# Masked softmax: later loads in quarter tiles of one packet per DMA engine, whole-tile stores, an earlier start of GpSimd's loads

## The chip, the cores and the metric

The kernel runs on one core of a Trainium2 chip. The metric is the device time of one execution in microseconds (us); the time of a kernel is the median of its runs. The profile of one execution gives a span a little shorter than that time (155.8 us for a run of 158.12 us), and all places in time below count from the span's start.

## The reference

```python
def setup_inputs():
    batch, heads, seq_q, seq_k = 16, 8, 256, 256
    return {"x": randn(batch, heads, seq_q, seq_k).astype(float32),
            "lengths": randint(seq_k // 2, seq_k, size=batch).astype(int32)}

def reference(x, lengths):
    result = np.zeros_like(x)
    for b in range(batch):
        length = lengths[b]
        masked = x[b, :, :, :length].copy()
        masked = masked - np.max(masked, axis=-1, keepdims=True)
        exp_masked = np.exp(masked)
        result[b, :, :, :length] = exp_masked / np.sum(exp_masked, axis=-1, keepdims=True)
    return result
```

It is a softmax over the first `length` columns of every row, with zeros in the rest. Each of the 16 batch entries has a length of its own. The data are always the same: the lengths are 188 233 229 243 195 252 165 210 222 180 209 157 159 199 214 248.

## The kernel before, in words

One batch entry is one tile: 8 x 256 = 2,048 rows of 256 floats, 2 MB. It lies in SBUF as 128 partitions of 16 rows (`nt`), so that a partition's 16 KB are contiguous in memory too, as long as the rows have their full width. `xt` has 12 slots for 16 tiles; tiles 12 to 15 reuse the slots of tiles 0 to 3. Everything is done in place in a slot.

**Loads.** SyncE issues the first four loads (`ahead = 4`), full width, before anything else. GpSimd issues the other twelve. It knows the length when the kernel runs, and `pick` branches down a tree to the narrowest of the prepared widths (160, 168, ..., 240, then 256) that covers it, so that columns which the mask would kill need not be read. What is then left of a row's 256 columns keeps zeros, which GpSimd's memsets (L133) wrote into slots 4 to 11. A narrow load reads 2,048 separate row pieces of `width` floats. A load of width 256 is contiguous in each partition. GpSimd's queue is opened by a wait for the landing of load 2 (L135), and a load into a slot that was used before waits for the stores of the older tile (L140).

**Compute.** For each tile, VectorE (DVE) waits for the load and takes the minimum with a `cap` vector that is hugely negative beyond the length (L182). ScalarE (ACT) takes exp of each of the 16 rows per partition, with the row's sum (L225). VectorE takes reciprocals of the sums (L207) and multiplies (L209), in two halves of 8 rows. VectorE does the minimum of tile b + 1 ahead of the multiplies of tile b.

**Stores.** SyncE stores each tile in three parts (L108): the first half as soon as its multiply is done, then, after the second multiply, two quarters. All stores stand in one queue with the first four loads, in program order. A semaphore per tile (or one for the last twelve) counts their landings.

The work is thus ordered by two DMA queues, that of SyncE (four loads, then 48 stores) and that of GpSimd (12 loads), which share 16 DMA engines.

Of the kernel before, what the change touches and what calls it, by code (L numbers as in the profile page):

```python
# [21 lines left out]
def kernel(  # L22
# [6 lines left out]
    nc = tc.nc  # L29
    P = nc.NUM_PARTITIONS  # L30

    batch, heads, seq_q, seq_k = x.shape
    rows = heads * seq_q
    assert rows % P == 0
    nt = rows // P
    half = nt // 2

    x_f = x.rearrange("b h q k -> b (h q) k").rearrange("b (p t) k -> b p t k", p=P)
    out_f = out.rearrange("b h q k -> b (h q) k").rearrange("b (p t) k -> b p t k", p=P)

    slots = min(12, batch)
    ahead = min(4, batch)

    widths = list(range(160, 248, 8))
    low = widths[0]

    parts = [slice(0, half), slice(half, half + half // 2), slice(half + half // 2, nt)]
    mid = seq_k // 2

    pool = ctx.enter_context(tc.tile_pool(name="all", bufs=1))  # L50
# [1 line left out]
    xt = pool.tile([P, slots, nt, seq_k], F32, name="xt")  # L52
    word64 = pool.tile([1, batch], mybir.dt.int64, name="word64")
# [14 lines left out]
    with tc.tile_critical(no_gpsimd_drain=True):  # L68
        sem = lambda n: ctx.enter_context(nc.semaphore(n))
        s_word = sem("s_word")  # L70
# [4 lines left out]
        s_ld = [sem(f"s_ld{b}") for b in range(batch)]  # L75

        early = batch - slots
        s_st = [sem(f"s_st{b}") for b in range(early)] + [sem("s_st")] * slots
# [5 lines left out]
        s_out = sem("s_out")  # L84

        def length(engine, b):

            return nc.values_load(  # L88
                (word_p if engine == POOL else word)[0:1, 2 * b : 2 * b + 1],
                engines=[engine],  # L90
                skip_runtime_bounds_check_because="compared with constants, never an address",
            )


        def load(engine, b, w):
            engine.dma_start(  # L96
                out=xt[:, b % slots, :, :w], in_=x_f[b, :, :, :w]
            ).then_inc(s_ld[b], 16)

        load(nc.sync, 0, seq_k)  # L100
        nc.scalar.dma_start(out=word64, in_=lengths[None, :]).then_inc(s_word, 16)
        for b in range(1, ahead):
            load(nc.sync, b, seq_k)
        for b in range(batch):
            for k, s in enumerate(parts):
                if k < 2:
                    nc.sync.wait_ge(s_out, 2 * b + k + 1)
                nc.sync.dma_start(  # L108
                    out=out_f[b, :, s, :], in_=xt[:, b % slots, s, :]
                ).then_inc(s_st[b], 16)  # L110
        nc.sync.wait_ge(s_st[-1], 16 * len(parts) * slots)

        def pick(v, b, ws):

            if len(ws) == 1:
                load(nc.gpsimd, b, ws[0])
                return
            m = (len(ws) - 1) // 2  # L120
            with nc.gpsimd.If(v <= ws[m]):  # L121
                pick(v, b, ws[: m + 1])
            with nc.gpsimd.Else():  # L123
                pick(v, b, ws[m + 1 :])
# [7 lines left out]
        for b in range(ahead, slots):  # L132
            nc.gpsimd.memset(xt[:, b, :, low:], 0.0).then_inc(s_fill, 1)  # L133
        nc.gpsimd.wait_ge(s_word_p, 16)
        nc.gpsimd.wait_ge(s_ld[ahead - 2], 16)  # L135
        for n in range(ahead, batch):
            if n < slots:
                nc.gpsimd.wait_ge(s_fill, n - ahead + 1)
            else:
                nc.gpsimd.wait_ge(s_st[n - slots], 16 * len(parts))  # L140
            pick(length(POOL, n), n, widths + [seq_k])


# [20 lines left out]
        def make_cap(b):  # L164

            step(
                nc.vector.tensor_scalar(  # L167
                    out=cap[:, b % 4, :],
                    in0=iota_h,
                    scalar1=len_s[:, b : b + 1],  # L170
                    scalar2=-1.0e30,
                    op0=ALU.subtract,
                    op1=ALU.mult,
                )
            )
            return v
# [3 lines left out]
        def clip(b, lo, hi):  # L180
            t = xt[:, b % slots]
            return nc.vector.tensor_tensor(  # L182
                out=t[:, :, lo:hi],
                in0=t[:, :, lo:hi],
                in1=cap[:, b % 4, None, lo:hi].to_broadcast([P, nt, hi - lo]),
                op=ALU.min,
            )

        def mask(b):
            if b + 1 < batch and b + 1 not in cap_at:  # L190
                cap_at[b + 1] = make_cap(b + 1)
            v_len = length(DVE, b)
            nc.vector.wait_ge(s_v, cap_at[b])
            nc.vector.wait_ge(s_ld[b], 16)  # L194
            with nc.vector.If(v_len < mid):  # L195
                clip(b, 0, mid)
            clip(b, mid, seq_k).then_inc(s_min, 1)

        mask(0)
        for b in range(batch):  # L200
            if b + 1 < batch:
                mask(b + 1)
            t = xt[:, b % slots]
            for h in range(2):
                s = slice(h * half, (h + 1) * half)
                nc.vector.wait_ge(s_exp, 2 * b + h + 1)
                step(nc.vector.reciprocal(out=inv_sum[:, b, s], in_=row_sum[:, b, s]))  # L207
                nc.vector.wait_ge(s_v, v)
                ins = nc.vector.tensor_tensor(  # L209
                    out=t[:, s, :],  # L210
                    in0=t[:, s, :],
                    in1=inv_sum[:, b, s, None].to_broadcast([P, half, seq_k]),
                    op=ALU.mult,
                )
                ins.then_inc(s_out, 1)
# [3 lines left out]
        for first, last in ((0, slots), (slots, batch)):  # L219
            with nc.Fori(first, last, 1, engines=[ACT]) as i:  # L220
                nc.scalar.wait_ge(s_min, i + 1)
                slot = i - first
                for j in range(nt):
                    e = xt[:, bass.ds(slot, 1), j, :]
                    ins = nc.scalar.activation(  # L225
                        out=e,
                        in_=e,
# [35 lines left out]
```

The softmax here doesn't subtract the row's maximum and nothing guards it: scores larger than these inputs give would overflow.

## Time and profile before

| | |
|---|---|
| time, median of 3 runs | 158.03 us (157.84 to 158.28) |
| span of the profile | 155.8 us |
| VectorE busy | 120.8 us (78%) |
| ScalarE busy | 105.3 us (68%) |
| GpSimd busy | 25.0 us (16%) |
| read from and written to HBM | 28.51 MB and 33.55 MB |

How to read it: a busy time is the sum of the instructions of an engine. The page also counts the packets of each DMA queue, with their bytes and the time that they took as a share of 16 engines' span: q1 is SyncE's queue and q0 GpSimd's. A packet is the piece of a transfer that one DMA engine handles in one turn. Completion signals of a DMA, of 4 bytes, are counted as packets too (those under 512 B). The time "to landing" of a DMA runs from its issue to its completion, and holds the time that it stood in its queue.

The costliest rows of the page's table of groups, with the busy time, the mean of one in ns, and the idle time before them with what ended it:

```profile
L225 ACT ACTIVATE xt<-xt x256 | 102.4, 402 | 26.6 <-DVE xt L182 26.6
L209 DVE TENSOR_TENSOR xt<-xt,inv_sum 128x2048 f32<-128x2048 f32 x32 | 73.3, 2292 | 1.1
...
L182 DVE TENSOR_TENSOR xt<-xt,cap 128x2048 f32<-128x2048 f32 x16 | 36.6, 2287 | 11.5 <-DMA xt<-in_x_dram 11.4
L96 POOL DMA_DIRECT2D xt<-in_x_dram x12 | 12.7, 1056 | 41.6 <-issue 41.5
L133 POOL MEMSET xt<- 128x1536 f32 x8 | 11.0, 1426 | 0.3 <-DVE iota_h L157 0.3
```

And the DMA issues, with KB of each and median us to landing:

```profile
out_dram<-xt SPq DMA_DIRECT2D x16, 1024.0 KB, 22.8
out_dram<-xt SPq DMA_DIRECT2D x32, 512.0 KB, 22.7
xt<-in_x_dram SPq DMA_DIRECT2D x4, 2048.0 KB, 14.4
xt<-in_x_dram POOLq DMA_DIRECT2D x3, 1728.0 KB, 54.0
```

### The profile page before, as it was taken

The numbers are of one execution on the slowest core, as the hardware profiler recorded it, in microseconds if no ns is written. First come the engines' busy times: TensorE is split into PE (matmuls) and PEld (weight loads), VectorE is DVE, ScalarE is ACT, GpSimd is POOL, SyncE is SP. The second block draws the span as 40 slices with busy tenths as digits, with TensorE's granted clock in tenths as the row PEclk, the third lists the DMA queues.
The fourth block names the chain that finished last, engine by engine and source line by source line (L and its number), as shares of the span: only waits on it lengthen the run. The fifth ranks groups of instructions, "written<-read, shape, count | busy, mean of one in ns | idle before, by whom it ended". The sixth has DMA issues, their size and how long they took to land.

```text
span 155.8 us, 1177 instructions
## 1 busy us (share of the span) xinstructions
PE 0.2 (0%) x1; PEld 0.1 (0%) x1; DVE 120.8 (78%) x99; ACT 105.3 (68%) x514; POOL 25.0 (16%) x27
## 2 busy tenths in 40 slices
PE   0000000000000000000000000000000000000000
PEld 0000000000000000000000000000000000000000
DVE  2566999999999999869995999997968999900000
ACT  3009999997979797929696597978692989200000
POOL 5995045742002002010000000000000000000000
DMA  5999999999999999999999999999999999999991
GB/s 126 421 446 421 437 357 386 411 444 426 378 401 405 414 418 412 419 408 405 422 408 414 407 415 408 407 417 409 422 438 426 409 428 413 424 427 428 425 411 50
DMA packets 11607, 62.11 MB, mean 399 GB/s; under 512 B 1058, under 2 KB 1154, under 8 KB 8786
## 3 DMA queue, kind: packets, MB, share of 16 engines
q1 hardware_dynamic: 7488, 41.95, 65.8%
q0 software_dynamic: 4112, 20.12, 32.1%
q14 instruction: 5, 0.04, 0.1%
q10 hardware_dynamic: 2, 0.00, 0.0%
HBM read 28.51 MB, written 33.55 MB: 398 GB/s over the span
## 4 chain that ended last, share of the span: by engine, by line
DMA 33%; DVE 29%; issue 12%; POOL 6%; another core or an unknown queue 4%; POOLq 2%; SPq 1%; DVEq 0%
DMA xt<-in_x_dram 33%; DVE xt L209 17%; DVE xt L182 10%; POOL xt L133 4%; POOL xt L96 2%; DVE inv_sum L207 1%; DVE cap L167 1%; POOLq L88 1%; POOLq L121 1%; SPq L96 1%; DVEq L195 0%; POOLq L123 0%; DVEq L194 0%; SPq L258 0%
## 5 line engine op out<-in xcount | busy, mean ns | idle before, releaser
L225 ACT ACTIVATE xt<-xt x256 | 102.4, 402 | 26.6 <-DVE xt L182 26.6
L209 DVE TENSOR_TENSOR xt<-xt,inv_sum 128x2048 f32<-128x2048 f32 x32 | 73.3, 2292 | 1.1
L225 ACT ACTIVATION_READ_ACCUMULATOR xt<-xt x256 | 48.0, 187 | 0.0
L182 DVE TENSOR_TENSOR xt<-xt,cap 128x2048 f32<-128x2048 f32 x16 | 36.6, 2287 | 11.5 <-DMA xt<-in_x_dram 11.4
L96 POOL DMA_DIRECT2D xt<-in_x_dram x12 | 12.7, 1056 | 41.6 <-issue 41.5
L133 POOL MEMSET xt<- 128x1536 f32 x8 | 11.0, 1426 | 0.3 <-DVE iota_h L157 0.3
L167 DVE TENSOR_SCALAR cap<-iota_h,len_s 128x256 f32<-128x256 f32 x16 | 8.5, 537 | 0.0
L207 DVE RECIPROCAL inv_sum<-row_sum 128x8 f32<-128x8 f32 x32 | 6.2, 195 | 0.0
L157 DVE TENSOR_SCALAR iota_h<-iota_i 128x256 f32<-128x256 int32 x1 | 0.3, 295 | 2.6 <-POOL iota_i L127 2.6
L218 ACT ACT_TABLE_LOAD x1 | 1.3, 1283 | 1.5 <-SPq L68 1.5
L126 POOL DMA_DIRECT2D word_p<-in_lengths_dram x1 | 0.6, 633 | 1.1 <-SPq L68 1.1
L161 DVE COPY len_s<-len_f 128x16 f32<-128x16 f32 x1 | 0.2, 175 | 0.4 <-PE len_f L146 0.4
L127 POOL IOTA iota_i<- 128x256 int32 x1 | 0.4, 360 | 0.1
L218 ACT ACTIVATE warm<-const-float32-0.0 128x1 f32<-128x1 f32 x1 | 0.2, 203 | 0.0
L130 POOL MEMSET ones<- 1x128 bf16 x1 | 0.2, 194 | 0.0
L146 PE MATMUL len_f<-len_b,ones 1*128 1x16 bf16 x1 | 0.2, 168 | 3.1 <-DVE len_b L159 3.1
L159 DVE CAST len_b<-word 1x16 bf16<-1x16 int32 x1 | 0.2, 155 | 0.0
L247 POOL MEMSET const-float32-0.0<- 128x1 f32 x1 | 0.1, 98 | 0.2 <-issue 0.2
L146 PEld LDWEIGHTS len_f<-len_b,ones 1*128 1x128 bf16 x1 | 0.1, 98 | 3.1 <-POOL ones L130 3.1
L247 POOL MEMSET const-bfloat16-1.0<- 128x1 bf16 x1 | 0.1, 99 | 0.0
L247 POOL MEMSET const-uint8-127<- 128x1 uint8 x1 | 0.1, 99 | 0.0
L247 POOL MEMSET const-float32-1.0<- 128x1 f32 x1 | 0.1, 98 | 0.0
## 6 DMA issues: line engine op xcount, KB each, us to landing
out_dram<-xt SPq DMA_DIRECT2D x16, 1024.0 KB, 22.8
out_dram<-xt SPq DMA_DIRECT2D x32, 512.0 KB, 22.7
xt<-in_x_dram SPq DMA_DIRECT2D x4, 2048.0 KB, 14.4
xt<-in_x_dram POOLq DMA_DIRECT2D x3, 1728.0 KB, 54.0
xt<-in_x_dram POOLq DMA_DIRECT2D x2, 2048.0 KB, 37.6
xt<-in_x_dram POOLq DMA_DIRECT2D x2, 1600.0 KB, 36.3
xt<-in_x_dram POOLq DMA_DIRECT2D x2, 1280.0 KB, 61.5
xt<-in_x_dram POOLq DMA_DIRECT2D x1, 1792.0 KB, 39.9
```

Source lines behind the costliest of these rows:

```text
L88: return nc.values_load((word_p if engine == POOL else word)[0:1, 2 * b : 2 * b + 1], engines=[engine], skip_runtime_bounds_check_because= ...
L96: engine.dma_start(out=xt[:, b % slots, :, :w], in_=x_f[b, :, :, :w]).then_inc(s_ld[b], 16)
L121: with nc.gpsimd.If(v <= ws[m]):
L126: nc.gpsimd.dma_start(out=word64_p, in_=lengths[None, :]).then_inc(s_word_p, 16)
L127: nc.gpsimd.iota(iota_i, pattern=[[1, seq_k]], base=0, channel_multiplier=0).then_inc(s_iota, 1)
L133: nc.gpsimd.memset(xt[:, b, :, low:], 0.0).then_inc(s_fill, 1)
L167: nc.vector.tensor_scalar(out=cap[:, b % 4, :], in0=iota_h, scalar1=len_s[:, b : b + 1], scalar2=-1.0e30, op0=ALU.subtract, op1=ALU.mult,)
L182: return nc.vector.tensor_tensor(out=t[:, :, lo:hi], in0=t[:, :, lo:hi], in1=cap[:, b % 4, None, lo:hi].to_broadcast([P, nt, hi - lo]), op ...
L207: step(nc.vector.reciprocal(out=inv_sum[:, b, s], in_=row_sum[:, b, s]))
L209: ins = nc.vector.tensor_tensor(out=t[:, s, :], in0=t[:, s, :], in1=inv_sum[:, b, s, None].to_broadcast([P, half, seq_k]), op=ALU.mult,)
L218: nc.scalar.activation(out=warm, in_=nc.const_aps.tensor(0.0, (P, 1), F32), func=EXP)
L225: ins = nc.scalar.activation(out=e, in_=e, func=EXP, accum_out=row_sum[:, bass.ds(i, 1), j],)
```

## The change

Four edits:

1. Each of GpSimd's loads becomes four DMAs of 4 rows per partition (a quarter tile), each with `single_packet=True`: what one DMA engine has to do for a quarter goes as one packet.
2. Stores go out as whole tiles, one DMA of 2 MB after the second multiply. Tiles 0 and 15 still go in two halves. The completion counts follow (a load is complete at 64, a tile's stores at 32).
3. GpSimd's queue opens at the landing of load 1 instead of load 2.
4. The prepared widths are 160 to 216 in steps of 8, then 232 and 256; 224 and 240 are left out. Of these lengths, only tile 8 (222) is loaded wider for it.

The purpose is to give the DMA engines fewer and larger packets, to let loads go ahead of stores, and to have GpSimd's loads under way before SyncE's first loads have run out.

```diff
-    widths = list(range(160, 248, 8))
+    widths = list(range(160, 224, 8)) + [232]
...
-    parts = [slice(0, half), slice(half, half + half // 2), slice(half + half // 2, nt)]
+    step = 4
+    pieces = nt // step
...
-        load(nc.sync, 0, seq_k)
-        nc.scalar.dma_start(out=word64, in_=lengths[None, :]).then_inc(s_word, 16)
-        for b in range(1, ahead):
-            load(nc.sync, b, seq_k)
+        for b in range(ahead):
+            nc.sync.dma_start(out=xt[:, b], in_=x_f[b]).then_inc(s_ld[b], 16 * pieces)
+            if b == 0:
+                nc.scalar.dma_start(out=word64, in_=lengths[None, :]).then_inc(s_word, 16)
         for b in range(batch):
-            for k, s in enumerate(parts):
-                if k < 2:
-                    nc.sync.wait_ge(s_out, 2 * b + k + 1)
-                nc.sync.dma_start(
-                    out=out_f[b, :, s, :], in_=xt[:, b % slots, s, :]
-                ).then_inc(s_st[b], 16)
-        nc.sync.wait_ge(s_st[-1], 16 * len(parts) * slots)
+            if b in (0, batch - 1):
+                for h in range(2):
+                    s = slice(h * half, (h + 1) * half)
+                    nc.sync.wait_ge(s_out, 2 * b + h + 1)
+                    nc.sync.dma_start(
+                        out=out_f[b, :, s, :], in_=xt[:, b % slots, s, :]
+                    ).then_inc(s_st[b], 16)
+            else:
+                nc.sync.wait_ge(s_out, 2 * b + 2)
+                nc.sync.dma_start(out=out_f[b], in_=xt[:, b % slots]).then_inc(s_st[b], 32)
+        nc.sync.wait_ge(s_st[-1], 32 * slots)
...
             if len(ws) == 1:
-                load(nc.gpsimd, b, ws[0])
+                for k in range(pieces):
+                    s = slice(k * step, (k + 1) * step)
+                    nc.gpsimd.dma_start(
+                        out=xt[:, b % slots, s, : ws[0]],
+                        in_=x_f[b, :, s, : ws[0]],
+                        single_packet=True,
+                    ).then_inc(s_ld[b], 16)
                 return
...
-        nc.gpsimd.wait_ge(s_ld[ahead - 2], 16)
+        nc.gpsimd.wait_ge(s_ld[ahead - 3], 16 * pieces)
```

More of the change, by code (lines that the diff above doesn't have):

```diff
@@ L92, in length @@
             )
[L95 to L98, printed above, removed]
-        load(nc.sync, 0, seq_k)
-        nc.scalar.dma_start(out=word64, in_=lengths[None, :]).then_inc(s_word, 16)
-        for b in range(1, ahead):
-            load(nc.sync, b, seq_k)
-        for b in range(batch):
-            for k, s in enumerate(parts):
-                if k < 2:
-                    nc.sync.wait_ge(s_out, 2 * b + k + 1)
-                nc.sync.dma_start(
-                    out=out_f[b, :, s, :], in_=xt[:, b % slots, s, :]
-                ).then_inc(s_st[b], 16)
-        nc.sync.wait_ge(s_st[-1], 16 * len(parts) * slots)
+        for b in range(ahead):
+            nc.sync.dma_start(out=xt[:, b], in_=x_f[b]).then_inc(s_ld[b], 16 * pieces)
+            if b == 0:
+                nc.scalar.dma_start(out=word64, in_=lengths[None, :]).then_inc(s_word, 16)
+        for b in range(batch):
+            if b in (0, batch - 1):
[9 more added lines that the diff above has]
+        nc.sync.wait_ge(s_st[-1], 32 * slots)
         def pick(v, b, ws):
             if len(ws) == 1:
-                load(nc.gpsimd, b, ws[0])
+                for k in range(pieces):
[5 more added lines that the diff above has]
+                    ).then_inc(s_ld[b], 16)
                 return
@@ L139 @@
             else:
-                nc.gpsimd.wait_ge(s_st[n - slots], 16 * len(parts))
+                nc.gpsimd.wait_ge(s_st[n - slots], 32)
             pick(length(POOL, n), n, widths + [seq_k])
@@ L193, in mask @@
             nc.vector.wait_ge(s_v, cap_at[b])
-            nc.vector.wait_ge(s_ld[b], 16)
+            nc.vector.wait_ge(s_ld[b], 16 * pieces)
             with nc.vector.If(v_len < mid):
```

## The prediction

> **What bounds the kernel now.** I read the page first: the span, the DMA totals and queues, the chain of waits. Then the table of windows, to see whether the DMA engines ever idle, and the DMA view of single stretches, for the cost of a packet; last the waits, for what VectorE has in hand.
>
> ```profile
> span 155.8 us, 1177 instructions
> ...
> DMA packets 11607, 62.11 MB, mean 399 GB/s; under 512 B 1058, under 2 KB 1154, under 8 KB 8786
> ...
> q1 hardware_dynamic: 7488, 41.95, 65.8%
> q0 software_dynamic: 4112, 20.12, 32.1%
> ```
>
> q1 is SyncE's queue (four first loads, all stores), q0 is GpSimd's (twelve later loads). Their packets took 65.8 + 32.1 = 97.9% of the time of 16 DMA engines. VectorE, the busiest compute engine, has 78%. So the DMA engines are the bound, and the question is what a packet costs them.
>
> ```profile
> 2.00:22.00 20.00, 0.17 (x1) 0.10 (x1) 14.71 (x14) 11.51 (x55) 13.01 (x13) 1.00 1.00 405
> 22.00:24.00 2.00, 0.00 (x0) 0.00 (x0) 1.97 (x3) 2.00 (x11) 0.38 (x1) 1.00 0.91 344
> 24.00:28.00 4.00, 0.00 (x0) 0.00 (x0) 3.97 (x3) 4.00 (x21) 2.82 (x3) 1.00 0.99 385
> 40.00:60.00 20.00, 0.00 (x0) 0.00 (x0) 19.66 (x17) 17.92 (x90) 2.30 (x2) 1.00 1.02 406
> 60.00:80.00 20.00, 0.00 (x0) 0.00 (x0) 17.41 (x15) 14.98 (x74) 0.56 (x1) 1.00 1.02 413
> ```
>
> The last two columns are the DMA share and GB/s. The share is 1.0 nearly everywhere; only around 22 to 28 us, where the first loads are done and GpSimd's have hardly begun, does the rate sag.
>
> ```profile
> DMA packets 149, 2.18 MB, mean 436 GB/s; under 512 B 16, under 2 KB 16, under 8 KB 16
> ...
> q1 hardware_dynamic: 149, 2.18, 101.8%
> ```
>
> That is 10 to 15 us: only full loads, in 16 KB packets. And 60 to 80 us, stores of 8 and 4 KB packets beside narrow loads of 4 to 5 KB packets:
>
> ```profile
> DMA packets 1842, 8.25 MB, mean 413 GB/s; under 512 B 131, under 2 KB 147, under 8 KB 1586
> ...
> q1 hardware_dynamic: 921, 4.42, 54.3%
> q0 software_dynamic: 921, 3.84, 47.8%
> ```
>
> Both queues sent exactly 921 packets: the engines alternate packet by packet. The price of a packet comes out of these two stretches. First: 1.018 x 16 engines x 5 us = 81.4 us of engine time for 149 packets, 0.546 us each, at 14.6 KB on average. Second: 1.021 x 16 x 20 = 326.7 us for 1,842 packets, 0.177 us each, at 4.48 KB. The difference, 0.369 us over 10.15 KB, is 0.0364 ns per byte; what is left, 0.177 - 0.163, is 14 ns per packet. Test on the whole run: 11,607 x 14 ns / 16 = 10.2 us, plus 62.11 MB x 0.0364 / 16 = 141.3 us, together 151.5 us; the page's 97.9% of 155.8 is 152.5 us. So the line holds within 1 us, and about 10 us of this kernel is cost per packet.
>
> ```profile
> DVE xt L182 <- DMA xt<-in_x_dram: 11.4, 7, 3.0
> ```
>
> VectorE waits 11.4 us in all for loads, and its last multiply begins at 134.1 and ends at 136.4 us. Stores then drain until about 153.7. Compute could end near 136.4 - 11.4 = 125 us: it has over 17 us in hand.
>
> **What the Trainium skill says.** DMA: Bandwidth & Descriptors, "Queues, rings and completion order", says that each DMA engine goes round robin over its queue rows and switches only at packet boundaries; the equal counts of 921 agree. Its section "SWDGE vs HWDGE vs iDMA" has packets of preferably at most 4,096 B and at most 64 descriptors: GpSimd's narrow packets here average 3.84 MB / 921 = 4.2 KB, completions counted in, which agrees with the size. A quarter tile puts 8 partitions x 4 rows = 32 row pieces on an engine, under the 64. "Why small descriptors are slow (HBM only)" gives a fixed cost of about three cycles per packet and calls joining descriptors worthwhile only at 256 B or less. That speaks against the change; the trace's 14 ns per packet speaks for it, and I go with the trace.
>
> **The change part by part.**
>
> Stores. Before, each tile goes out as 128 packets of 8 KB and 256 of 4 KB: 384 x 16 = 6,144. Now 14 tiles go whole, as 128 pieces of 16 KB per tile (the size that the full loads show), and two tiles as 256 of 8 KB: 1,792 + 512 = 2,304. Removed: 3,840 x 14 ns / 16 = 3.4 us of every engine's time. As the engines are the bound, all of it counts. A whole-tile store leaves one 2.29 us multiply (L209) later than the first half did; loads and older stores fill that time. Tile 15 keeps its halves, so the end does not wait longer.
>
> Loads. GpSimd's ten narrow and two full loads are now 3,888 data packets (4,112 on q0 less the completions of 12 loads and the lengths, about 16 each, and some 16 small records at the start). Then they are 12 x 4 x 16 = 768, of 20.19 MB / 768 = 26 KB. If 14 ns go with each, 3,120 x 14 / 16 = 2.7 us. What the trace cannot show: all narrow packets have nearly one size, so whether their cost is per packet, or per row piece of 640 to 928 bytes, is not separable. In the first case the gain is 2.7 us, in the second 0. I take two thirds, 1.8 us.
>
> Small additions. Tile 8 (length 222) is loaded 232 wide instead of 224: 2,048 rows x 32 B = 65 KB, 0.15 us. Completions: 48 loads x 16 on q0 instead of 12 x 16, on q1 22 x 16 instead of 52 x 16: a net 96 more, under 0.1 us. The larger increments of 64 and 32 add no packet of data.
>
> GpSimd's issue. The page gives 1,056 ns on average for one load issue (540 the least, 1,197 the most); four are 2.2 to 4.8 us per tile, with about 0.6 us of branches. At 62% of the bandwidth (below), a 1.68 MB tile takes 1.68 / 0.26 = 6.5 us. So issue keeps ahead, and what is queued behind it on GpSimd is only the next load.
>
> Opening at the second landing. GpSimd's eight memsets end at 14.0 us, and load 1 lands at about 13.8, when the clip of tile 1 begins; so the wait falls from 18.6 to 14.0 us. The first issue followed the release by 1.5 us, and the first data of q0 came between 25 and 30 us. Now they come between 16 and 21, and the sag is filled: (413 - 344) / 413 x 2 + (413 - 385) / 413 x 4 = 0.6 us gained. The price: packets of 26 KB alternate with 16 KB ones, so loads get 26 / (26 + 16) = 62%. Loads 2 and 3 and store 0 stand in q1 and get 38%. If q0 starts at 16 us, some 2.4 MB of q1 remain, and load 3 lands near 16 + 2.4 / 0.16 = 31 us, where its clip (28.7 us now) waits 2 us. Store 0 follows at about 43 us, so the reload of its slot, issued at 36.0 now, moves back by 7 us. Behind both is VectorE; 2 us out of over 17 are hidden, and the DMA engines work on something else meanwhile.
>
> Sum: 3.4 + 1.8 + 0.6 - 0.2 = 5.6 us. 158.0 - 5.6 = 152.4 us.
>
> **The rivals.**
>
> Stores alone gain: the load packets' cost sticks to the row pieces. Then 3.4 - 0.2 + 0.3 to 0.6 remain, and the time is 154.3. For it: the rows are short and the page named above knows a cost per descriptor; against: in 60 to 80 us q0's packets took 0.478 x 320 / 921 = 0.166 us for 4.17 KB, exactly the common line, although each holds several rows.
>
> Everything gains: 14 ns off every packet and the whole sag, 3.4 + 2.7 + 0.6 - 0.2 = 6.5 us, so 151.5. Below that is little room: at the 435 GB/s that the page has as the fabric's ceiling, 62.18 MB take 142.9 us, plus 2 us before and 2 us after the data; that would be 149 with the 2.2 us by which the times exceed the span.
>
> Slower: a large packet stalls. If an engine in a 26 KB packet waits once for the memory, with nothing else to switch to, at the 0.2 us that the same page's "Latency and other measured facts" gives for an HBM access (an estimate), then 48 packets per engine cost 9.6 us, and the time is 158.0 - 5.6 + 9.6 = 162. Against it: 16 KB packets run back to back at 436 GB/s. For it: no packet here is larger than 16 KB, and nothing shows the mixture of large reads and large writes.
>
> No change: the mixed rate of 406 to 418 GB/s comes from reading and writing HBM at once, not from packets; 158. Against: the stores alone, from 125 to 140 us, run at 423 with 4.8 KB per packet, on the same line (0.186 us measured, 0.190 worked out).
>
> An idle gap from compute I give almost nothing: it would take more than 17 us of new waits of VectorE.
>
> **How the numbers follow.** Central case (151 to 153.7): 0.52. Stores alone (153.7 to 156.5): 0.23. Better than 151: 0.08. No change: 0.05. Slower: 0.12. Faster by more than 0.3%, that is below 157.5, gathers the first three, 0.83; same 0.05; slower 0.12. The range takes in both bounds of the load packets and the sag, and goes to 149.9 and 156.0, which leaves out about 2 in 10.
>
> **What would show it.** Right: q0 with about 1,550 packets, q1 with about 3,200; a DMA share still near 1.0 up to the end, at 420 to 430 GB/s in mixed stretches; no sag at 22 to 28 us; q0 taking about 60% while both queues are full; loads landing earlier and VectorE ending before 136 us. Wrong: mixed stretches still at 406 to 413 GB/s with larger packets (the cost was not per packet), or a DMA share well under 1 in the middle or at the end (a stall, or stores that come too late).

## The result, and the profile after

| | before | after |
|---|---|---|
| time, median of 4 runs each | 157.94 us | 169.86 us |
| ratio, with 95% interval | | 1.0758 (1.0707 to 1.081) |
| span of the profile | 155.8 us | 168.9 us |
| VectorE's waits for loads | 11.4 us | 33.2 us |
| start of VectorE's last clip (minimum, tile 15) | 124.4 us | 146.7 us |

The change makes the kernel slower by 11.9 us, where 5.6 us less were predicted. The last clips, before and after, in the list of VectorE's instructions (start and duration in us):

```profile
124.36 2.29 DVE L182 TENSOR_TENSOR xt<-xt,cap 128x2048 f32<-128x2048 f32 x1
146.74 2.29 DVE L188 TENSOR_TENSOR xt<-xt,cap 128x2048 f32<-128x2048 f32 x1 [2.66 <-DMA xt<-in_x_dram]
```

From the page after, the DMA rows in 40 slices, the totals and the queues:

```profile
span 168.9 us, 1179 instructions
...
DMA  5999999999999999999999999999999997744990
GB/s 140 435 423 435 414 304 426 426 427 427 413 446 365 324 349 340 406 417 410 412 396 369 422 367 422 363 426 392 407 404 374 418 428 301 319 194 186 394 413 0
DMA packets 8906, 62.20 MB, mean 368 GB/s; under 512 B 1154, under 2 KB 1602, under 8 KB 6082
...
q1 hardware_dynamic: 3168, 41.94, 59.4%
q0 software_dynamic: 5728, 20.19, 33.6%
```

q1 has the 3,168 packets that were worked out, and it takes less engine time: 59.4% of 168.9 is 100.3 us, against 102.5 before. But q0 has 5,728 packets, more than before (4,112) and not about 1,550. Its engine time rises from 50.0 to 56.7 us. Two more things are new: near the end the DMA engines stand idle, and from the 13th to the 16th slice (of 4.2 us each) they are busy at 324 to 365 GB/s only.

Who gets the engines while both queues are full is read from the DMA view of 94 to 98 us of the kernel after:

```profile
DMA packets 170, 1.68 MB, mean 420 GB/s; under 512 B 15, under 2 KB 16, under 8 KB 85
...
q1 hardware_dynamic: 85, 1.39, 81.7%
q0 software_dynamic: 85, 0.29, 18.0%
```

The two queues sent 85 packets each: they alternate, as before. But a store's turn is now 16 KB and a load's 3.4 KB with completions counted, so loads get 0.29 / 1.68 = 17% of the bytes. The prediction had 62%. VectorE then runs out of loaded tiles. In the list of waits of the kernel after (us in total, times, longest):

```profile
ACT xt L231 <- DVE xt L188: 49.0, 14, 12.6
DVE xt L188 <- DMA xt<-in_x_dram: 33.2, 12, 11.4
...
SPq L110 <- DVE xt L215: 127.7, 14, 18.7
...
SPq L97 <- DMA out_dram<-xt: 6.0, 1, 6.0
SPq L264 <- PEq L264: 2.9, 2, 2.5
```

The longest wait for a load, 11.4 us, is the one before the clip of tile 5, a full-width tile. The same two rows of SyncE in the kernel before:

```profile
SPq L96 <- DMA out_dram<-xt: 16.2, 1, 16.2
SPq L258 <- PEq L258: 1.0, 2, 0.6
```

SyncE's wait for the last stores was 16.2 us before, with a queue full of stores; now it is 6.0 us, and stores go out as VectorE makes them. The last row is a wait of SyncE at the very end, called its last wait below; it was 1.0 us before and is 2.9 us now.

The table of windows of the kernel after shows the end (the last two columns are the DMA share and GB/s):

```profile
137.00:142.00 5.00, 0.00 (x0) 0.00 (x0) 4.93 (x5) 2.57 (x13) 0.00 (x0) 1.00 0.97 413
142.00:146.00 4.00, 0.00 (x0) 0.00 (x0) 2.09 (x1) 3.92 (x20) 0.00 (x0) 1.00 0.47 199
146.00:150.00 4.00, 0.00 (x0) 0.00 (x0) 3.22 (x3) 0.75 (x4) 0.00 (x0) 1.00 0.94 397
150.00:154.00 4.00, 0.00 (x0) 0.00 (x0) 3.96 (x4) 4.00 (x22) 0.00 (x0) 1.00 0.01 4
154.00:159.00 5.00, 0.00 (x0) 0.00 (x0) 4.72 (x4) 1.75 (x10) 0.00 (x0) 1.00 0.87 367
```

Between 150 and 154 us VectorE works without a break and the DMA engines have nothing to do: the stores of the last tiles are not ready. The end now follows from the last load through VectorE, not from the bytes.

From 54 to 67 us q0 is alone. VectorE multiplies tile 4 only after the clip of tile 5, and that clip had to wait for its load until 55.9 us, so that the next store is issued only at 63.1 us; its first data come at 67.4. The view of 55 to 65 us:

```profile
DMA packets 944, 3.35 MB, mean 335 GB/s; under 512 B 127, under 2 KB 220, under 8 KB 943
...
q0 software_dynamic: 943, 3.35, 102.8%
```

The engines are fully busy at 335 GB/s. Here narrow loads alone move fewer bytes in a microsecond than narrow loads mixed with stores.

The profile is of the slowest of the four executions, 170.66 us. Its span is 13.1 us longer than before, and this splits as follows. The packets' engine time rose by 157.1 - 152.5 = 4.5 us (q0 +6.7, q1 -2.2). The time not filled by packets rose from 3.3 to 11.8 us, by 8.5: the longer last wait accounts for 1.9 of them, and idle engines for want of stores for most of the rest. The cutting-up of the loads explains little of q0's 6.7 us: with it alone, in the kernel before, q0 takes 31.1% of 163.2 us, 50.8 us, which is 0.8 more than before. With the whole-tile stores alone it takes 32.8% of 161.3 us, 52.9 us, although the loads are as before.

### The profile page after: what moved, and what is told of

It reads as the page before. It is cut to its first block, busy times and chain, and to the rows that moved or that the text cites. A ratio compares the mean times of both kernels' runs of the same rounds, so it can differ in the third digit from the quotient of the medians.

```text
span 168.9 us, 1179 instructions
## 1 busy us (share of the span) xinstructions
PE 0.2 (0%) x1; PEld 0.1 (0%) x1; DVE 121.5 (72%) x99; ACT 105.2 (62%) x514; POOL 46.4 (27%) x63
## 3 DMA queue, kind: packets, MB, share of 16 engines
q1 hardware_dynamic: 3168, 41.94, 59.4%
q0 software_dynamic: 5728, 20.19, 33.6%
## 4 chain that ended last, share of the span: by engine, by line
DVE 41%; DMA 25%; issue 11%; another core or an unknown queue 10%; POOL 6%; DVEq 1%; SPq 0%; POOLq 0%
DMA xt<-in_x_dram 25%; DVE xt L215 23%; DVE xt L188 15%; POOL xt L139 4%; POOL xt L120 2%; DVE cap L173 2%; DVE inv_sum L213 2%; DVEq L201 0%; SPq L97 0%; POOLq L127 0%; DVEq L200 0%; POOLq L89 0%; SPq L264 0%; SPq L69 0%
## 5 line engine op out<-in xcount | busy, mean ns | idle before, releaser
L188 DVE TENSOR_TENSOR xt<-xt,cap 128x2048 f32<-128x2048 f32 x16 | 36.6, 2289 | 33.2 <-DMA xt<-in_x_dram 33.2
L120 POOL DMA_DIRECT2D xt<-in_x_dram x48 | 34.1, 716 | 21.3 <-issue 21.0
```

Of the source, the lines that this page charges most:

```text
L120: nc.gpsimd.dma_start(out=xt[:, b % slots, s, : ws[0]], in_=x_f[b, :, s, : ws[0]], single_packet=True,).then_inc(s_ld[b], 16)
L188: return nc.vector.tensor_tensor(out=t[:, :, lo:hi], in0=t[:, :, lo:hi], in1=cap[:, b % 4, None, lo:hi].to_broadcast([P, nt, hi - lo]), op ...
```

## The experiments

The "turns theory", as the expectations call it: the DMA engines take one packet of each queue in turn, whatever its size, so a queue's progress is counted in turns, and a turn of the loads lasts as long as the packet of the other queue lets it. The end is the later of two things: the engines' total time, or VectorE's last clip plus some 20 us (18 to 22, as the tables below show). Rivals were the flag, the later issue of the stores, the cutting-up of the loads as such, and the opening. The fourth edit, the widths, was not run alone.

All experiments are timed against the kernel before, in 3 rounds where nothing else is said. After each text of what was expected stands the time, then its ratio to the kernel before, with the 95% interval in brackets. Cuts in the code are marked with three dots. "Last clip" is the start of VectorE's minimum of tile 15 in the profile.

**Without the flag.** The changed kernel with one line less:

```diff
-                        single_packet=True,
```

> The changed kernel without single_packet on GpSimd's quarter loads. Turns theory: the flag joins nothing (q0's records average 4.1 KB in the changed kernel), the two queues still alternate packet by packet, and what costs the time are the 16 KB store packets. Then the time stays within 1% of the changed kernel's 169.9 us, and q0 keeps about 5,700 packets. Flag theory: the flag does act, and holds the loads back (waits, reads in one go). Then without it the time falls towards 158 us, and a narrow q0 packet takes less than in the changed kernel. If the flag acts and helps, the time rises above 172 us.

The time is 170.15 us, 1.0751 (1.0713 to 1.079): that of the changed kernel. q0 again has 5,728 packets, which take 33.5% of the engines' span. The flag changed nothing that the trace or the time shows. The flag theory falls.

**Quarter stores at the same moment.** The changed kernel with each whole-tile store cut into four DMAs, issued where the whole one was; the completion counts follow.

```diff
...
-                nc.sync.dma_start(out=out_f[b], in_=xt[:, b % slots]).then_inc(s_st[b], 32)
+                for k in range(pieces):
+                    s = slice(k * 4, (k + 1) * 4)
+                    nc.sync.dma_start(
+                        out=out_f[b, :, s, :], in_=xt[:, b % slots, s, :]
+                    ).then_inc(s_st[b], 16)
...
```

> The changed kernel with each of the fourteen whole-tile stores issued at the same point, after the second multiply, but as four DMAs of 4 rows per partition (4 KB packets). Turns theory: with packets of 4 KB on both sides the loads get about half the bandwidth again instead of a fifth, VectorE's waits for loads fall from 33 us to under 15 us, and the time comes to 155 to 159 us. Late-store theory: the loss comes from stores that are issued only after the second multiply, so that slots come free later; then the time stays near 169 us. Load theory: the loss comes from quarter loads and GpSimd's 48 issues; then it stays near 169 us too.

The time is 162.91 us, 1.0319 (1.029 to 1.0347). VectorE's waits fall to 15.1 us, the last clip comes at 128.5. The DMA view of 60 to 80 us of this kernel:

```profile
q1 hardware_dynamic: 1131, 4.11, 51.6%
q0 software_dynamic: 1133, 3.99, 50.7%
```

Half the bytes go to the loads, as expected. 7 of the 11.9 us are won back by the packet size alone, at an unchanged moment of issue, which refutes the late-store theory as the main cause. It does not show that late stores cost nothing: with a last clip as early as this the end does not depend on them (see the tables of last clip and span). But 162.9 is not 155 to 159: something of the loads is left.

**Only the whole-tile stores.** The kernel before with the stores of the changed one.

> The kernel before with only the stores of the changed one (whole tiles, tiles 0 and 15 in halves); loads stay one DMA per tile, the queue opens at load 2. Turns theory: the loads' share falls to about 4.4 / (4.4 + 16.4), a fifth, wherever a store is queued, and the time is 165 to 171 us, with VectorE waiting 25 us or more. Load theory (quarter loads or the flag cost the time): about 155 us, 3 us better than before, as the fewer store packets alone would give.

The time is 162.27 us, 1.0265 (1.0244 to 1.0286): slower, as the turns theory has it, but by less than I expected. VectorE waits 27.1 us, and the last clip comes at 141.2. The loads get a fifth only while a store is queued. From 60 to 80 us q1 sent 288 packets and q0 919, and the loads had 3.77 of 7.97 MB: a VectorE that waits for loads makes no stores. So the change has two harmful parts: the stores, 4.2 us alone, and the quarter loads.

**Opening at load 2.** The changed kernel with `s_ld[ahead - 2]`.

> The changed kernel with GpSimd's queue opened at the landing of load 2 again. Turns theory: the opening hardly matters, as the loads get a fifth of the turns either way: 168 to 172 us, and if anything later loads make it slower by 1 to 2 us. Opening theory: early loads of q0 hold up loads 2 and 3 and store 0 and upset the order from there; then undoing it brings the time to 165 us or less.

The time is 169.36 us, 1.0728 (1.0691 to 1.0765). The opening does not matter for the loss.

**Only the quarter loads.** The kernel before with the quarter loads in `pick`.

> The kernel before with only the quarter loads of the changed one, flag included; stores in three parts, queue opened at load 2, all widths. Turns theory: q0's packets become 4,928 data packets instead of 3,888 and 576 more completions, about 1,600 x 14 ns / 16 = 1.4 us for every DMA engine, and the two full-width loads (tiles 5 and 15) fall from 16 KB to 4 KB a turn, so that VectorE waits longer at tile 5; 159 to 161 us, and nothing is gained anywhere. Prediction's theory (one packet per engine and quarter): 155 to 156.5 us.

The time is 164.85 us, 1.0413 (1.0385 to 1.0442). The direction is that of the turns theory, but its size is missed by 4 us. q0 has 5,728 packets, so 358 turns per engine instead of 257; VectorE waits 30.5 us, and the last clip comes at 143.3. With the 4.2 us of the stores alone, the 6.8 us here make 11.0 of the 11.9 us; the rest is left for the opening, the widths and what the parts do together. The windows of this kernel show the loss at the end:

```profile
138.00:142.00 4.00, 0.00 (x0) 0.00 (x0) 0.83 (x1) 2.66 (x14) 0.00 (x0) 1.00 1.01 419
142.00:146.00 4.00, 0.00 (x0) 0.00 (x0) 2.69 (x3) 0.21 (x1) 0.00 (x0) 1.00 0.26 108
146.00:148.00 2.00, 0.00 (x0) 0.00 (x0) 2.00 (x2) 2.00 (x11) 0.00 (x0) 1.00 0.02 8
```

**Full-width loads left whole**, in the changed kernel:

```diff
+            if ws == [seq_k]:
+                nc.gpsimd.dma_start(
+                    out=xt[:, b % slots], in_=x_f[b]
+                ).then_inc(s_ld[b], 16 * pieces)
+                return
```

> The changed kernel, but a load of full width (tiles 5 and 15) stays one DMA, of 16 KB packets. Turns theory: these two loads again get half the turns' bytes beside 16 KB stores; the wait of 11.4 us before tile 5's clip falls to about 3 us, VectorE's waits fall from 33 to about 25 us, and the time to 163 to 166 us. Narrow-piece theory (what costs is that the ten narrow loads are cut up): it stays above 168 us.

The time is 166.39 us, 1.0529 (1.0509 to 1.0548), just above what was expected. q0 has 864 packets fewer, and the kernel is 3.5 us faster than the changed one. The wait before tile 5's clip falls from 11.4 to 2.9 us. But VectorE's waits for loads in all stay at 30.1 us, where about 25 were expected: later loads are waited for longer. As whole loads the two full-width tiles go in 16 KB packets; in quarters a partition's piece is only 4 KB long, and they need four times as many turns.

**A dose of store size.** The kernel before with two halves per tile:

```diff
-    parts = [slice(0, half), slice(half, half + half // 2), slice(half + half // 2, nt)]
+    parts = [slice(0, half), slice(half, nt)]
```

> The kernel before with every tile stored in two halves (8 KB packets), a dose between before and whole tiles. Turns theory: 2,048 store packets fewer save 1.8 us of every DMA engine, but the loads' share falls to about 4.4 / 12.6, a third; VectorE waits 18 to 24 us for loads instead of 11; 156.5 to 160 us, well under the 162.3 us of whole tiles. If only the count of packets mattered: 156.2 us. If only the late issue of a whole tile's store cost the time (the halves are issued as early as before): 156.2 us as well, with waits as before.

The time is 158.14 us, 1.0018 (0.9998 to 1.0038): the same as before. Single executions lie between 157.80 and 159.72 us. Waits are 23.6 us and the last clip comes at 137.8 us: there are fewer packets, and the loads are just not too late. From 60 to 80 us the loads had 3.06 of 8.38 MB, a bit over a third, with 734 packets to 729. Neither "only the packet count" nor "only the issue time" fits, as both had the waits unchanged or 156.2 us.

**Large stores late.** The kernel before, with large stores only for late tiles:

```diff
...
+            if b in range(12, batch - 1):
+                nc.sync.wait_ge(s_out, 2 * b + 2)
+                nc.sync.dma_start(out=out_f[b], in_=xt[:, b % slots]).then_inc(s_st[b], 48)
+                continue
-            for k, s in enumerate(parts):
+            for k, s in enumerate(parts if b < 10 else halves):
...
```

> The kernel before, with large stores only where few loads are left to hold up: tiles 0 to 9 as before, 10, 11 and 15 in halves, 12 to 14 whole. Turns theory: 1,152 packets fewer are 1.0 us of every DMA engine, and VectorE's waits stay within 3 us of before's 11.4: 156.5 to 157.6 us, faster than both kernels. If late stores or large packets cost by themselves, whatever stands beside them: 158 us or more.

The time is 157.56 us, 0.9972 (0.9953 to 0.9991), at the upper edge of what was expected. VectorE waits 9.2 us.

The next four ran in 5 rounds. The first stores halves from tile 8 and whole tiles from tile 11:

> The kernel before with tiles 0 to 7 stored as before, 8 to 10 and 15 in halves, 11 to 14 whole. Turns theory: 1,536 store packets fewer, 1.3 us of every DMA engine, and VectorE's last clip, at 124 us before, stays under 134 us, so that the drain still sets the end: 156.7 to 157.6 us. If large packets help nothing by themselves: 158 us.

The time is 157.48 us, 0.9968 (0.9956 to 0.9981): faster than the kernel before, by half a microsecond. The second stores halves from tile 4:

> The kernel before with tiles 0 to 3 stored as before, 4 to 10 and 15 in halves, 11 to 14 whole. Turns theory: 2,048 packets fewer, 1.8 us of every DMA engine; the loads of tiles 12 to 15 meet 8 KB packets, VectorE's last clip comes at 128 to 136 us, just early enough: 156.3 to 157.6 us. If the last clip comes after 137 us, the end follows it by about 20 us, and it is 158 us or more.

The time is 161.67 us, 1.0242 (1.0221 to 1.0263). Its last clip comes at 139.1 us, after the 137 named. It has 512 store packets fewer than the run before it and is 4 us slower. The packets' total time is the same (95.2% of 159.3 and 97.6% of 155.1 us, 151.7 and 151.4), but the engines have to wait for stores.

**Quarter stores in the kernel before.**

> The kernel before with every store in four quarters of 4 KB packets. The count of packets alone: 2,048 more store packets at 14 ns are 1.8 us of every DMA engine, with the completions 1.9: 160.0 us. The share: loads get half the bandwidth in every turn, VectorE's last clip moves forward to 121 to 124 us and its waits for loads fall below 11 us, but the drain sets the end, so that this brings nothing. If the loads' share were all that counts, also in this kernel, it would be faster than 158.

The time is 158.91 us, 1.0057 (1.0038 to 1.0076). Waits fall to 4.0 us and the last clip moves forward to 116.3 us, further than expected, and the kernel is slower all the same: where the engines are the bound, earlier loads buy nothing and packets cost. But they cost less than expected. q1's share is 66.3% of 156.6 = 103.8 us, 1.3 more than before, for 2,304 packets with completions: 1.3 x 16 / 2,304 = 9 ns each, not 14. In half stores, with 2,304 fewer, q1 takes 65.3% of 155.7 us, 0.8 us less than before, or 6 ns each.

**Only the opening at load 1**, in the kernel before.

> The kernel before with only the opening of GpSimd's queue moved to the landing of load 1. Prediction's step: the sag of 22 to 28 us is filled, 0.6 us gained, 157.5 us. Rival: the sag stays, as in the changed kernel, whose rate falls to 300 GB/s there although its q0 was open: 158 us, no change within 0.3%.

The time is 158.22 us, 1.0014 (1.0002 to 1.0027): there is no gain. Its windows:

```profile
20.00:22.00 2.00, 0.00 (x0) 0.00 (x0) 2.00 (x3) 2.00 (x11) 1.80 (x2) 1.00 0.97 403
22.00:24.00 2.00, 0.00 (x0) 0.00 (x0) 1.97 (x3) 2.00 (x11) 1.11 (x2) 1.00 1.02 295
24.00:28.00 4.00, 0.00 (x0) 0.00 (x0) 3.97 (x3) 4.00 (x21) 2.40 (x3) 1.00 0.97 397
```

The sag is still there, with a share of 1.02: packets take longer in that stretch, so more queued work does not fill it.

**What of the quarter loads costs what.** Two runs, in 3 rounds again. Half loads (`range(2)`, 8 rows each):

> The kernel before with GpSimd's loads as two DMAs of 8 rows per partition (24 instead of 12). Turns theory: 262 data packets and 24 completions per DMA engine on q0 instead of 243 and 12; at the 0.2 us by which each of the 101 extra turns of the quarter loads moved the last load, it lands 6 us later, near 128 us, and VectorE's last clip stays before 136, where the drain sets the end. The rest is 31 turns of about 12 ns, 0.4 us, and at the end 12 more GpSimd DMAs at 0.053 us (1.9 us for 36), 0.6 us: 159.1 us, 158.6 to 159.8. If the cost were per GpSimd DMA throughout (6.8 us for 36), 160.4 us.

The time is 159.34 us, 1.0083 (1.0064 to 1.0103), within the turns theory's range. The last load's data end at 129.5 us, the last clip is at 130.4, and q0 has 4,608 packets. Then only the ten narrow loads in quarters:

> The kernel before with quarter loads for the ten narrow tiles alone; the two full-width loads stay one DMA of 16 KB packets. Turns theory: 47 more turns of q0 instead of 101, the last load lands near 131 us and the last clip before 136, so the drain sets the end: 0.5 us of turns and 1.6 us at the end for 30 more GpSimd DMAs, 160.2 us, 159.5 to 161. If cutting the narrow loads were the cost, it stays near 164 us, and SyncE's last wait near 2.7 us.

The time is 162.23 us, 1.0267 (1.0242 to 1.0292): 2 us above the expectation. The last clip is at 135.2, before 136, as expected, so the total drain should have set the end. The windows of this kernel at its end:

```profile
150.00:152.00 2.00, 0.00 (x0) 0.00 (x0) 0.00 (x0) 0.00 (x0) 0.00 (x0) 1.00 1.03 422
152.00:154.00 2.00, 0.00 (x0) 0.00 (x0) 0.00 (x0) 0.00 (x0) 0.00 (x0) 1.00 0.29 119
154.00:157.00 3.00, 0.00 (x0) 0.00 (x0) 0.00 (x0) 0.00 (x0) 0.00 (x0) 1.00 0.05 22
```

At 152.5 us fewer than half of the engines still move data. From about 154.2 us on the trace's records of packets (each has a start, a duration and a size) follow one another singly, end to end, until 156.6 us: one engine of 16 works on, which is the share of 0.05. In the kernel before the data end at 153.6 us. And SyncE's last wait, in the lists of waits of half loads and of this kernel, in this order:

```profile
SPq L264 <- PEq L264: 1.6, 2, 1.2
```

```profile
SPq L267 <- PEq L267: 2.7, 2, 2.3
```

It is 1.0 us with 12 loads of GpSimd (0.6 in one kernel, quarter stores in the kernel before), 1.6 with 24, 2.7 with 42 and 2.9 with 48: about 0.05 us more for each. So the 4.6 us by which this kernel's span is longer are a longer last wait (1.7 us) and data that end some 3 us later, for the most part with few engines still at work. Where the full-width loads are cut too, a last clip that comes too late is added.

**Last clip and span** of the profiles, in us, first with GpSimd's loads whole, then cut up (without the run that only lacks the flag):

| loads whole | last clip | span |
|---|---|---|
| quarter stores in the kernel before | 116.3 | 156.6 |
| opening at load 1 in the kernel before | 121.7 | 155.9 |
| large stores from tile 10 | 123.7 | 155.8 |
| before | 124.4 | 155.8 |
| large stores from tile 8 | 127.0 | 155.1 |
| half stores | 137.8 | 155.7 |
| large stores from tile 4 | 139.1 | 159.3 |
| whole stores only | 141.2 | 161.3 |

| loads cut up | last clip | span |
|---|---|---|
| changed, quarter stores | 128.5 | 160.8 |
| half loads | 130.4 | 157.6 |
| narrow quarters only | 135.2 | 160.4 |
| quarter loads only | 143.3 | 163.2 |
| changed, full width whole | 143.5 | 165.4 |
| changed, opening at load 2 | 145.3 | 167.4 |
| changed | 146.7 | 168.9 |

The profiles of whole stores only and of full width whole are of executions 1.4 and 1.1 us slower than the median of their kernel.

With whole loads the span does not depend on the last clip down to half stores: the engines' total time sets it. Half stores stand at the corner itself: their engines are idle for a moment (a DMA share of 0.78 from 142 to 146 us), and the span is still that of before. With a later last clip the engines run out of work, and the end follows the last clip at a fixed distance. By the trace's records of packets the stored data end 15.8 and 15.9 us after the last clip in half stores and quarter loads only, which store tile 14 in parts. They end 18.1 us after it in the five kernels of the tables with a late clip that store tile 14 whole. VectorE clips tile 15 before it multiplies tile 14, and a whole store then waits for tile 14's second multiply, which ends 2.4 us after the first. So the later issue of this one store costs about 2.2 us where the last clip sets the end, in whole stores only as in the changed kernel. This is worked out from these runs; none tried that store alone. After the data come 2.1 us with 12 loads of GpSimd and 3.8 to 4.0 with 42 or 48, which makes the 18 to 22 us between last clip and span.

As the data end at 153.6 us in the kernel before, the corner lies at a last clip near 138 us with tile 14 in parts, and near 135.5 with it whole. With cut loads the kernels of an early last clip stand 2 to 5 us above 155.8, for the reasons just named and, in the first of them, 154.9 us of packets' time (64.4 + 31.9% of 160.8) instead of 152.5.

## Why the prediction was wrong, point by point

**What bounds the kernel before**: right. The engines' time sets its end, and VectorE has slack. The quarter stores in the kernel before, with waits of 4.0 instead of 11.4 us, gain nothing.

**The failing step is the one on the loads**: "Then they are 12 x 4 x 16 = 768, of 20.19 MB / 768 = 26 KB." The flag's name was taken for its effect, in the description of the change as well. The runs show 4,928 data packets and 768 completions, the same with and without the flag. In the trace's records a narrow packet holds rows until 4,096 bytes are reached, before and after: five rows of 864 bytes (4,320), seven of 640 (4,480), a little above the 4,096 that the prediction names as preferred. The 32 row pieces that an engine has of a quarter of the first kind so go as six packets of five rows and one of two. The prediction had set its 32 pieces against the limit of 64, and had read an average of 4.2 KB from its own trace, but did not set its 26 KB against that size. Of the two ends that the step kept open (2.7 us gained or 0) neither was an end: the load packets' engine time rose by 6.7 us. That a quarter of a full-width tile has only 4 KB contiguous per partition stood in the shapes, and its four times as many turns were not counted.

**The share, 62% for the loads**, followed from it by the right rule and the wrong size. The rule of the Trainium skill, DMA: Bandwidth & Descriptors, "Queues, rings and completion order", that an engine goes round robin packet by packet, agrees with the trace in the stretches where both queues were full, with 85 to 85 and 1,131 to 1,133. With 3.4 and 16 KB it says 17%, which the trace shows.

**"An idle gap from compute I give almost nothing"** failed too. With the loads at a fifth while stores were queued, the slack was used up. It was also smaller than the 17 us: the last clip could move by some 13 us (124.4 to about 138), and by 11 with tile 14 stored whole, since after the last clip there are 12 us of VectorE's work and the last store's way out. The prediction did name the sign, a DMA share well under 1 at the end from stores that come too late.

**"Tile 15 keeps its halves, so the end does not wait longer"** was wrong as well: the end waits for tile 14, about 2.2 us.

**Stores, 3.4 us**: the engine time was right in sign and too large, as q1's fell by 2.2 us in the changed kernel. The price of 14 ns came from two stretches that differed in loads as well as in packet size; for stores alone it is 6 to 9 ns (half stores, quarter stores in the kernel before). But that "all of it counts" failed outright: with these stores alone the kernel is 4.2 us slower, as they take the loads' share.

**Opening and sag, 0.6 us**: nothing was gained, as the run with the opening alone shows. The low rate stays there with a DMA share of 1.02, so want of work was not what held it down; why packets take longer there is open. The harm expected for loads 2 and 3, hidden by slack, is not seen in the time either.

**GpSimd's issue keeps ahead**: right for the flow (716 ns on average, 48 issues), and incomplete: the last wait is longer by 0.05 us for each load DMA more.

**The rival "slower"** had the right sign with a wrong mechanism, a stall within packets of 26 KB; none exist, so its being nearest to the result was luck. The rival with stores alone gaining 3.4 us is refuted by whole-tile stores alone, 4.2 us slower.

## What to carry to other kernels

When two DMA queues compete, count turns, not bytes: while both are full, enlarging the packets of one takes bandwidth from the other in proportion. So large packets belong to the queue that the end depends on (leaving the two full-width loads whole gained 3.5 us here), or to the stretch in which the other queue is nearly empty (which gained 0.5 us). Read packet counts in a trace before trusting a flag's name, and work out from the access pattern how many contiguous bytes a piece has after a tile is cut. A slack that hides a small delay is finite: locate the corner (here a last clip between 135 and 138 us) before calling a wait hidden.

## What the runs showed of the hardware that was not expected

- `single_packet=True` on GpSimd's loads left the recorded packets and the time unchanged (5,728 packets; 170.15 us without it, 169.86 with it).
- On the narrow loads, a packet holds whole rows until 4,096 bytes are reached (4,320 to 4,800 bytes here, by the records of packets); a full-width load of 16 rows goes in packets of 16,384.
- Narrow loads alone move 335 GB/s with the engines fully busy (55 to 65 us of the changed kernel); mixed with 4 KB stores the engines reach 406 GB/s. With whole loads the low rate is seen too, though less, where q0 is alone in whole stores only:

```profile
58.00:59.50 1.50, 0.00 (x0) 0.00 (x0) 0.06 (x1) 0.20 (x2) 0.04 (x1) 1.00 1.03 364
66.00:69.00 3.00, 0.00 (x0) 0.00 (x0) 0.94 (x3) 2.38 (x12) 0.07 (x1) 1.00 1.01 384
```

So it does not come from the cutting alone. Why is not settled.
- A whole-tile store that was issued into an empty q1 had its first data after 0.8 us where q0 was idle or on its last engine (144.1 and 153.9 us of the changed kernel), and after 4.4 and 3.7 us where q0 kept all 16 engines busy (63.1 and 88.6 us). The cause was not tried.
- SyncE's last wait grows by about 0.05 us for each load DMA of GpSimd, from 1.0 us at 12 to 2.9 us at 48. The cause was not tried.
- With cut-up loads, and with whole-tile stores, the engines drift apart. The 16 completion signals of the last load come within 2.2 us before, 6.2 in whole stores only, 9.0 in quarter loads only and 8.6 in the changed kernel, and VectorE waits for the last. In quarter loads only q0 moved only 0.10 MB from 135 to 142 us, next to a full q1:

```profile
q1 hardware_dynamic: 624, 2.82, 97.3%
q0 software_dynamic: 29, 0.10, 3.4%
```

From 136.5 us on the records of packets show q0's packets one at a time, for the most part 0.3 us apart, so a single lagging engine fits, as it does at the end of the run with narrow quarters. The trace does not name engines, so which one and why stays open. It is part of why quarter loads cost more than expected.
